# Moving the first block's GpSimd element-wise work to ScalarE and VectorE in a two-block fp32 kernel

## The chip, the cores and the metric

One core of one Trainium2 chip. The metric is the device time of one execution in microseconds (us); the kernel before took 2739.27 us (median of 3 runs, 2730.82 to 2743.38).

## What is computed

Two transformer-like blocks over 256 tokens of width 1024, in float32. The first block has two layers; each has three recurrent mixers (hgrn2 with 8 heads, retention with 8 heads, rwkv7 with 16 heads), every one of them run forwards and backwards, then three gated projections that are summed, and a residual. The second block has feed-forward layers, a short convolution and two kinds of attention; the change does not touch it. The part of the reference that matters here, cut:

```
for l in range(2):
    h = rmsnorm(x, norm_g[l])
    a_q, a_ff, ..., c_s, c_g, merge = split(h @ w_in[l])
    y_a = hgrn2_mixer(...) * silu(a_g)
    y_b = retention_mixer(...) * silu(b_g)      # head_groupnorm(o, g, b)
    y_c = rwkv7_mixer(...) * silu(c_g)          # head_groupnorm(o, ln_g, ln_b) + bonus
    gates = sigmoid(merge)
    mixed = gates_0*(y_a@w_a) + gates_1*(y_b@w_b) + gates_2*(y_c@w_c)
    x = x + mixed @ w_out[l]
```

## The kernel before

All large products are made at float32 accuracy out of three passes with split operands. `wload` (L350) brings 512 KB of weights into a `raw` tile over SP's queue; for each 128x512 piece ScalarE writes the rounded high part (`whi`, L411) and VectorE the rest (`wlo`, L412), and TensorE multiplies low by high, high by low and high by high (L370 to L372), 128x256 at a time. Such pieces have 4 pairs of buffers, and 1 more in the first block.

In the first block this stream of weights is the *fill*, and the recurrent mixers run beside it as chains of small steps. `weave` (L46) decides at build time when each chain's next step is written into the program, from written-down estimates of how long a step takes; then a scheduler sets the order of each engine's queue. Every engine works through its queue in order, so an instruction that waits holds up all that stand behind it. The chains are:

- rwkv7: 8 pairs of heads per layer. `rwkv_operands` makes the decays `eL`, `enL`, the keys `bk`, their decayed copy `bkP` and the sum `sqr` (called `ks` in the code) of both directions' keys; `rwkv_scores` makes `ar`, `UV`, the bonus `bv`, the score matrices `SCa`, `SCr` and their inverse (`XY`, `W`, `X`); `rwkv_states` runs the recurrence; `rwkv_out` makes the norm.
- hgrn2 and retention: `hgrn_pair`, `hgrn_head` and `ret_pair`, 4 pairs per layer each.
- `branch` multiplies a mixer's output by its projection and adds it to `mixed` (tile `gate`). After the last branch `layer` splits `mixed` into `hb` for the product with `w_out`.

GpSimd has, per layer: two copies `Pc` per rwkv7 pair (L957, L958), the sum `sqr` (L969), the two products `bkP` (L977), two copies each of `ar` and `UV` (through a helper, L105), the sum `onr` + `bv` (L1198); for hgrn2 `kf` (L1239 in layer 1, L1242 in layer 0), the product `EK` (L1292), two sums into `cm` (L1330, L1331) and four into `P` (L1351); for retention the gain and bias of the norm `ro` (L1440); and the sum into `mixed` (L895).

Of the kernel before, what the change touches and what calls it, by code (L numbers as in the profile page):

```python
# [13 lines left out]
AF = mybir.ActivationFunctionType  # L14
ALU = mybir.AluOpType
# [506 lines left out]
class First(Core):  # L522
# [355 lines left out]
    def branch(s, l, b, j, c, ys, st, parts=False):  # L878


        nc = s.nc
        sl = slice(2 * j, 2 * j + 2)
        gt, mixed = s.gates(b, j, st), st["gate", 0]
        p = s.bank("pb")
        if parts:
            yield from s.fm(p, c[:1], ys, open=True)
            yield from s.fm(p, c[1:], ys, cont=True)
        else:
            yield from s.fm(p, c, ys)
        if b == 0:  # L890
            nc.vector.scalar_tensor_tensor(gt, gt, 1.0, p, ALU.add, ALU.mult)
        else:
            t = s.tmp.tile([128, 2, T], F32, tag="gt", name="gb", bufs=1)
            nc.vector.scalar_tensor_tensor(t, gt, 1.0, p, ALU.add, ALU.mult)
            nc.gpsimd.tensor_tensor(mixed[:, sl, :], mixed[:, sl, :], t, ALU.add)  # L895

    def sums(s, out, fwd, bwd, n):

# [6 lines left out]
    def rwkv_operands(s, l, p, r, k, v, codes, out):  # L905
# [6 lines left out]
        col = lambda n: s.P(f"{n}{l}", p)  # L912
# [41 lines left out]
        A.activation(eL, csv, AF.Exp, scale=-EC)  # L954
        A.activation(enL, csv, AF.Exp, scale=EC)
        Pc = rp.tile([128, 2, 4], F32, tag="Pc", name="Pc", bufs=3)
        G.tensor_copy(Pc[:, 0, :], eL[:, 0, :, 63])  # L957
        G.tensor_copy(Pc[:, 1, :], eL[:, 1, :, 0])  # L958
        c4 = lambda t: t.rearrange("p (c t) -> p c t", c=4)
        bd = lambda t: c4(t).unsqueeze(1).to_broadcast([128, 2, 4, 64])  # L960
        bt = rp.tile([128, 2, 4, 64], F32, tag="cs", name="bt")
# [4 lines left out]
        A.activation(kd, ta4, AF.Identity, scale=s.ka1[l][:, 0, p:p + 1], bias=s.ka1[l][:, 1, p:p + 1])  # L966
        tt(kd, kd, bd(k), ALU.mult)
        ks = t1("sqr", 1)
        G.tensor_tensor(c4(ks), kd[:, 0], kd[:, 1], ALU.add)  # L969
        stt(ks, ks, col("rk"), r, ALU.mult, ALU.mult)  # L970
        stt(bk[:, :, :, 0, :], bt, -0.5, enL, ALU.mult, ALU.mult)
        A.copy(bk[64:128, :, :, 2, :], bk[64:128, :, :, 0, :])
# [1 line left out]

        bkP = rp.tile([128, 2, 3, 2, 64], F32, tag="A4", name="bkP")
        for d in range(2):
            G.tensor_tensor(bkP[:, d], bk[:, d, d:d + 3, 0:2, :],  # L977
                            Pc[:, d, d:d + 3].unsqueeze(2).unsqueeze(3).to_broadcast([128, 3, 2, 64]), ALU.mult)
        yield 220, 6000
        out[p] = vc, nkk, eL, Pc, bk, bkP, ks  # L980

    def rwkv_scores(s, l, p, r, v, ins, ev, wait):
# [3 lines left out]
        mm = nc.tensor.matmul  # L986
        tt = V.tensor_tensor
        vc, nkk, eL, Pc, bk, bkP, ks = ins
        c4 = lambda t: t.rearrange("p (c t) -> p c t", c=4)
        bd = lambda t: c4(t).unsqueeze(1).to_broadcast([128, 2, 4, 64])  # L990
        ar = rp.tile([128, 2, 4, 2, 64], F32, tag="ar", name="ar", bufs=2)
        n4 = c4(nkk)
        tt(ar[:, 0, :, 0, 1:], n4[:, :, 1:], eL[:, 0, :, :63], ALU.mult)
        G.tensor_copy(ar[:, 0, :, 0, 0:1], n4[:, :, 0:1])
        tt(ar[:, 1, :, 0, :63], n4[:, :, :63], eL[:, 1, :, 1:], ALU.mult)
        G.tensor_copy(ar[:, 1, :, 0, 63:64], n4[:, :, 63:64])
        tt(ar[:, :, :, 1, :], bd(r), eL, ALU.mult)
        ev.add(("r used", p))

# [1 line left out]
        for h in range(2):  # L1001
            o = (1 - h) * 64
            for i in range(2):
                A.copy(UV[o:o + 64, 0, i::2, h, :], vc[i * 64:i * 64 + 64, :, h, :])
            G.tensor_copy(UV[o:o + 64, 1, :, h, :], UV[o:o + 64, 0, :, h, :])
        yield wait
        bv = rp.tile([128, T], F32, tag="bv", name="bv", bufs=2)
        pb = mp.tile([128, T], F32, tag="m", name="pb")
        mm(out=pb, lhsT=s.blk, rhs=ks, start=True, stop=True)
        tt(bv, pb, v, ALU.mult)  # L1010
        ev.add(("v used", p))
        yield 480, 2500

# [172 lines left out]
    def rwkv_out(s, l, p, ins, cg):  # L1186

        V, tt = s.nc.vector, s.nc.vector.tensor_tensor
        on, sq, bv = ins
        col = lambda n: s.P(f"{n}{l}", p)  # L1190
        r4 = s.rp.tile([128, 4, 64], F32, tag="sqe", name="wide", bufs=1)
        s.columns(s.colps[:, 4:8], [[sq]], 2, 64.0, 64e-5, "rsr", out=r4)
        yield 220, 4000
        y = s.spread_wide(s.mps.tile([128, T], F32, tag="m", name="pn"), r4)
        yield 220, 0
        tt(on, on, y, ALU.mult)
        V.tensor_scalar(on, on, col("lg"), col("lb"), ALU.mult, ALU.add)
        s.nc.gpsimd.tensor_tensor(on, on, bv, ALU.add)  # L1198
        V.scalar_tensor_tensor(s.yc[:, p, :], on, 0.5, cg, ALU.mult, ALU.mult)


# [24 lines left out]
    def hgrn_pair(s, l, j, x, ys, ev):  # L1226
        nc, hp = s.nc, s.hp
        V, A = nc.vector, nc.scalar
        mm = nc.tensor.matmul
        has = lambda n: lambda: n in x  # L1230
        yield has("lf")
        lf = x["lf"]
        kf = hp.tile([128, 2, 2, T], F32, tag="kf", name="kf")
        for d, f in enumerate(lf):
            if l > 0:
                for h in range(2):
                    i = 8 * d + 2 * j + h
                    lb, om, nom = (s.lbc[:, m, i:i + 1] for m in range(3))
                    nc.gpsimd.tensor_scalar(kf[:, h, d, :], f[:, h, :], nom, om, ALU.mult, ALU.add)  # L1239
                    A.activation(f[:, h, :], f[:, h, :], AF.Identity, scale=om, bias=lb)  # L1240
            else:
                nc.gpsimd.tensor_scalar(kf[:, :, d, :], f, -0.5, 0.5, ALU.mult, ALU.add)  # L1242
                V.tensor_scalar(f, f, 0.5, 0.5, ALU.mult, ALU.add)
            V.tensor_scalar(f, f, 1e-6, None, ALU.max)
            A.activation(f, f, AF.Ln)
        yield 0, 4000
        po = s.hops.tile([128, 2, T], F32, tag="oh", name="hpo")
        for h in range(2):
            P = yield from s.hgrn_head(x, h, kf[:, h], [f[:, h, :] for f in lf], j, ev)
            yield has("v")  # L1250
            for jt in range(2):
                mm(out=po[:, h, :], lhsT=x["v"][:, h, jt, :], rhs=P[:, jt, :], start=jt == 0, stop=jt == 1)
            yield 860, 1000
        ev.add(("v used", j))
        sq = hp.tile([128, 2, T], F32, tag="Z", name="sqo")
        A.activation(sq, po, AF.Square)
        r = s.hmps.tile([128, 2, T], F32, tag="mh", name="hpn")
        c = s.columns(r.rearrange("p h t -> p (h t)"), [[sq[:, 0, :]], [sq[:, 1, :]]], 1, 128.0, 1e-6)
        yield 860, 3500
        s.spread(r, c, 1)  # L1260
        yield 440, 0
        y = hp.tile([128, 2, T], F32, tag="E", name="yo")
        for h in range(2):
            A.mul(y[:, h, :], po[:, h, :], s.P(f"hn{l}", 2 * j + h))
        yield has("g")
        g = x["g"]
        V.tensor_tensor(y, y, r, ALU.mult)
        V.scalar_tensor_tensor(y, y, 0.5, g, ALU.mult, ALU.mult)
        s.split(ys[0][:, 2 * j:2 * j + 2, :], ys[1][:, 2 * j:2 * j + 2, :], y)

    def hgrn_head(s, x, h, kf, lf, j, ev):
# [17 lines left out]
        EK = hp.tile([128, 2, T], F32, tag="Z", name="EK")  # L1289
        A.activation(EK, D, AF.Exp, scale=-1.0)  # L1290
        A.activation(D, D, AF.Exp, bias=s.eps[-SH])
        nc.gpsimd.tensor_tensor(EK, kf, EK, ALU.mult)  # L1292
        tt(D, q.unsqueeze(1).to_broadcast([128, 2, T]), D, ALU.mult)
        yield 0, 5500
        for d in range(2):
# [7 lines left out]
        for n in (8, 16, 32, 64, 128):  # L1303
# [21 lines left out]
            if n == 8:  # L1325
                for b in range(8):
                    sl, pp = slice(b * 32, b * 32 + 32), (b % 4) * 32
                    mm(out=pc[pp:pp + 32, b // 4, 0, :], lhsT=Z[:, 0, sl], rhs=Z[:, 1, sl], start=True, stop=True)
                tt(cm, pc, C["mh"].unsqueeze(1).to_broadcast([128, 2, 3, 32]), ALU.mult)
                nc.gpsimd.tensor_tensor(cm[:, :, 0, :], cm[:, :, 0, :], cm[:, :, 1, :], ALU.add)  # L1330
                nc.gpsimd.tensor_tensor(cm[:, :, 0, :], cm[:, :, 0, :], cm[:, :, 2, :], ALU.add)  # L1331
                pt = mp.tile([128, 2, T], F32, tag="mh", name="ppt")
            elif n == 16:
                for b in range(8):
                    sl, pp = slice(b * 32, b * 32 + 32), (b % 4) * 32
                    mm(out=pt[pp:pp + 32, b // 4, sl], lhsT=Z[:, 0, sl], rhs=Z[:, 1, sl], start=True, stop=True)
                yield 440, 0
            else:
                for b in range(g):
                    e, o = b * 2 * n, b * 2 * n + n  # L1340
                    for j0, i0 in ((e, o), (o, e)):
                        mm(out=pt[j0 % 128:j0 % 128 + n, j0 // 128, i0:i0 + n], lhsT=Z[:, 0, j0:j0 + n],
                           rhs=Z[:, 1, i0:i0 + n], start=True, stop=True)
                yield 440, 0
# [46 lines left out]
    def ret_pair(s, l, j, ins, st, new, ev):  # L1391
# [42 lines left out]
        for e in range(2):  # L1434
# [2 lines left out]
            tt(o[:, e], o[:, e], y[:, e, :].unsqueeze(1).to_broadcast([128, 2, T]), ALU.mult)  # L1437
            for vt in range(2):
                i = 2 * hd + vt
                G.tensor_scalar(o[:, e, vt, :], o[:, e, vt, :], s.P(f"rg{l}", i), s.P(f"rb{l}", i), ALU.mult, ALU.add)  # L1440
            V.scalar_tensor_tensor(o[:, e], o[:, e], 0.5, gt, ALU.mult, ALU.mult)
            b = (2 * hd) % 8
            s.split(ys[0][:, b:b + 2, :], ys[1][:, b:b + 2, :], o[:, e])
# [461 lines left out]
```

## Time and profile before

| what | value |
|---|---|
| median of 3 runs | 2739.27 us |
| the profiled execution | 2742.64 us, its span 2740.8 us |
| TensorE busy (matmul) | 2636.6 us, 96% |
| VectorE busy | 2068.3 us, 75% |
| ScalarE busy | 1494.7 us, 55% |
| GpSimd busy | 283.6 us, 10% |
| mean granted TensorE clock | 0.979 |

The first layer lies at about 0 to 850 us of the span, the second at 850 to 1700 us, the second block behind it. In the first 550 us of each layer the recurrent mixers run beside the weights (called the dense stages below, 50 to 550 us and 900 to 1400 us); behind them retention and the branches run beside the weights.

### The profile page before, as it was taken

Reading aid. Unit: us, or ns where it says so; the run is one execution under the profiler, and the core shown is the slowest. Engines: PE = TensorE matmul, PEld = TensorE weight load, DVE = VectorE, ACT = ScalarE, POOL = GpSimd, SP = SyncE. Lnnn points to the kernel's source line nnn. Section 1 sums busy time; section 2 is a strip of 40 time slices with the busy share of each in tenths; the row PEclk is TensorE's granted clock in tenths of the full one; section 3 lists DMA queues with packets and bytes.
Section 4 is the critical chain, followed back from the end, with each engine's and each line's share of the span. In section 5 each row is a group of like instructions: output and inputs, shape, how many; then the busy total and the mean of one; then the engine's idle time right before and its main releaser. Section 6 shows DMA issues by size and latency. Waiting matters only on the chain.

```text
span 2740.8 us, 76128 instructions
## 1 busy us (share of the span) xinstructions
PE 2636.6 (96%) x31971; PEld 2499.4 (91%) x31971; DVE 2068.3 (75%) x4578; ACT 1494.7 (55%) x2968; POOL 283.6 (10%) x385
## 2 busy tenths in 40 slices
PE   7999999999999899999999999999999999999999
PEld 7888888899999888888799999999999999987999
DVE  8988889866668988898967677766776767756665
ACT  6665646444456665656444455555555555554554
POOL 1111112101021222212100111000000000000000
PEclk9998999999999999999999999999999999998999
DMA  5332222244556332223245555556455655542555
GB/s 178 111 105 75 98 76 83 94 150 151 179 171 197 112 106 84 93 80 100 73 133 163 173 165 197 184 171 187 151 181 182 185 180 163 170 132 76 173 182 161
DMA packets 111800, 385.38 MB, mean 141 GB/s; under 512 B 12384, under 2 KB 16992, under 8 KB 111200
## 3 DMA queue, kind: packets, MB, share of 16 engines
q1 hardware_dynamic: 111024, 379.86, 42.9%
q8 instruction: 251, 4.11, 0.6%
q10 hardware_dynamic: 432, 0.64, 0.1%
q14 instruction: 93, 0.76, 0.1%
HBM read 378.36 MB, written 2.10 MB: 139 GB/s over the span
## 4 chain that ended last, share of the span: by engine, by line
PE 76%; DVE 16%; ACT 3%; issue 2%; POOL 1%; DMA 1%; SPq 0%; ACTq 0%; DVEq 0%; POOLq 0%
PE pj L370 7%; PE pj L372 6%; PE pj L371 6%; PE pg L370 4%; PE pg L372 4%; PE pg L371 4%; DVE wlo L412 4%; PE pw L370 3%; PE pw L372 3%; PE pw L371 3%; PE pu L370 3%; PE pu L372 3%; PE pu L371 3%; PE pb L370 2%; PE pb L371 2%; PE pb L372 2%
## 5 line engine op out<-in xcount | busy, mean ns | idle before, releaser
L411 ACT CAST whi<-raw 128x512 fp32r<-128x512 f32 (+1 forms) x1407 | 862.0, 618 | 825.3 <-PE pj L372 228.0
L412 DVE TENSOR_TENSOR wlo<-raw,whi 128x512 fp32r<-128x512 f32 (+1 forms) x1407 | 984.8, 707 | 422.0 <-ACT whi L411 412.4
L370 PE MATMUL pj<-hb,wlo 128*128 128x256 f32 x1408 | 425.3, 302 | 7.5 <-DVE wlo L412 7.1
L372 PE MATMUL pj<-hb,whi 128*128 128x256 f32 x1408 | 405.0, 288 | 0.0
L371 PE MATMUL pj<-hb,whi 128*128 128x256 f32 x1408 | 404.3, 287 | 0.0
L370 PEld LDWEIGHTS pj<-hb,wlo 128*128 128x128 f32 x1408 | 271.4, 193 | 19.5 <-DVE wlo L412 6.7
L371 PEld LDWEIGHTS pj<-hb,whi 128*128 128x128 f32 x1408 | 271.9, 193 | 1.9 <-issue 0.2
L372 PEld LDWEIGHTS pj<-hb,whi 128*128 128x128 f32 x1408 | 271.6, 193 | 1.4 <-issue 0.2
L371 PE MATMUL pg<-hs,whi 128*128 128x256 f32 x704 | 200.3, 284 | 2.0 <-DVE hs L499 2.0
L370 PE MATMUL pg<-hs,wlo 128*128 128x256 f32 x704 | 200.2, 284 | 1.5 <-DVE x L518 1.5
L370 PE MATMUL pu<-hs,wlo 128*128 128x256 f32 x704 | 199.9, 284 | 1.8 <-DVE wlo L412 1.6
L370 PE MATMUL pw<-g,wlo 128*128 128x256 f32 x704 | 199.6, 284 | 0.7 <-DVE wlo L412 0.7
L372 PE MATMUL pg<-hs,whi 128*128 128x256 f32 x704 | 200.2, 284 | 0.0
L372 PE MATMUL pu<-hs,whi 128*128 128x256 f32 x704 | 199.6, 283 | 0.0
L371 PE MATMUL pu<-hs,whi 128*128 128x256 f32 x704 | 199.3, 283 | 0.0
L371 PE MATMUL pw<-g,whi 128*128 128x256 f32 x704 | 199.2, 283 | 0.0
L372 PE MATMUL pw<-g,whi 128*128 128x256 f32 x704 | 199.2, 283 | 0.0
L370 PE MATMUL pb<-hs,wlo 128*128 128x256 f32 x512 | 145.3, 284 | 0.0
L371 PE MATMUL pb<-hs,whi 128*128 128x256 f32 x512 | 144.6, 282 | 0.0
L372 PE MATMUL pb<-hs,whi 128*128 128x256 f32 x512 | 144.6, 282 | 0.0
L371 PEld LDWEIGHTS pg<-hs,whi 128*128 128x128 f32 x704 | 135.7, 193 | 2.2 <-DVE hs L499 2.2
L370 PEld LDWEIGHTS pu<-hs,wlo 128*128 128x128 f32 x704 | 135.0, 192 | 2.6 <-DVE wlo L412 2.4
(526 smaller groups left out, 6852.8 us busy)
## 6 DMA issues: line engine op xcount, KB each, us to landing
raw<-in_win SPq DMA_DIRECT2D x292, 512.0 KB, 3.6
raw<-in_w SPq DMA_DIRECT2D x256, 512.0 KB, 3.6
raw<-in_wbb SPq DMA_DIRECT2D x32, 512.0 KB, 3.6
raw<-in_wo SPq DMA_DIRECT2D x32, 512.0 KB, 3.5
raw<-in_wconv SPq DMA_DIRECT2D x20, 512.0 KB, 3.6
raw<-in_wba SPq DMA_DIRECT2D x16, 512.0 KB, 3.5
raw<-in_wbc SPq DMA_DIRECT2D x16, 512.0 KB, 3.5
raw<-in_lora SPq DMA_DIRECT2D x16, 256.0 KB, 2.6
```

What stands on the lines that cost most here:

```text
L370: mm(out=out, lhsT=al, rhs=bh, start=start, stop=False)
L371: mm(out=out, lhsT=ah, rhs=bl, start=False, stop=False)
L372: mm(out=out, lhsT=ah, rhs=bh, start=False, stop=stop)
L411: s.nc.scalar.copy(dh, src)
L412: (eng or s.nc.vector).tensor_tensor(dl, src, dh.bitcast(F32), ALU.subtract)
```

## The change

GpSimd keeps only its start-up work. Copies (`Pc`, `ar`, `UV`), `bkP`, `kf` and the gain and bias of `ro` become ScalarE activations; `bkP` is six 128x128 activations with a per-partition factor in place of two products of 128x384. The sums and products (`sqr`, `EK`, `cm`, `P`, `mixed`) become VectorE instructions. The norm's bias is added to `bv` on ScalarE, right after `bv` is made, so that gain and sum of `onr` become one VectorE instruction in place of one on VectorE and one on GpSimd.

```diff
 branch:
-            nc.gpsimd.tensor_tensor(mixed[:, sl, :], mixed[:, sl, :], t, ALU.add)
+            nc.vector.tensor_tensor(mixed[:, sl, :], mixed[:, sl, :], t, ALU.add)
 rwkv_operands:
-        G.tensor_copy(Pc[:, 0, :], eL[:, 0, :, 63])
-        G.tensor_copy(Pc[:, 1, :], eL[:, 1, :, 0])
+        A.copy(Pc[:, 0, :], eL[:, 0, :, 63])
+        A.copy(Pc[:, 1, :], eL[:, 1, :, 0])
-        G.tensor_tensor(c4(ks), kd[:, 0], kd[:, 1], ALU.add)
+        tt(c4(ks), kd[:, 0], kd[:, 1], ALU.add)
-            G.tensor_tensor(bkP[:, d], bk[:, d, d:d + 3, 0:2, :],
-                            Pc[:, d, d:d + 3].unsqueeze(2).unsqueeze(3).to_broadcast([128, 3, 2, 64]), ALU.mult)
+            for c in range(3):
+                A.mul(bkP[:, d, c], bk[:, d, d + c, 0:2, :], Pc[:, d, d + c:d + c + 1])
 rwkv_scores:
+        lb = s.P(f"lb{l}", p)
-        G.tensor_copy(ar[:, 0, :, 0, 0:1], n4[:, :, 0:1])
+        A.copy(ar[:, 0, :, 0, 0:1], n4[:, :, 0:1])
-        G.tensor_copy(ar[:, 1, :, 0, 63:64], n4[:, :, 63:64])
+        A.copy(ar[:, 1, :, 0, 63:64], n4[:, :, 63:64])
-            G.tensor_copy(UV[o:o + 64, 1, :, h, :], UV[o:o + 64, 0, :, h, :])
+            A.copy(UV[o:o + 64, 1, :, h, :], UV[o:o + 64, 0, :, h, :])
         tt(bv, pb, v, ALU.mult)
+        A.activation(bv, bv, AF.Identity, bias=lb)
 rwkv_out:
-        V.tensor_scalar(on, on, col("lg"), col("lb"), ALU.mult, ALU.add)
-        s.nc.gpsimd.tensor_tensor(on, on, bv, ALU.add)
+        V.scalar_tensor_tensor(on, on, col("lg"), bv, ALU.mult, ALU.add)
 hgrn_pair:
-                    nc.gpsimd.tensor_scalar(kf[:, h, d, :], f[:, h, :], nom, om, ALU.mult, ALU.add)
+                    A.activation(kf[:, h, d, :], f[:, h, :], AF.Identity, scale=nom, bias=om)
-                nc.gpsimd.tensor_scalar(kf[:, :, d, :], f, -0.5, 0.5, ALU.mult, ALU.add)
+                A.activation(kf[:, :, d, :], f, AF.Copy, scale=-0.5, bias=0.5)
 hgrn_head:
-        nc.gpsimd.tensor_tensor(EK, kf, EK, ALU.mult)
+        tt(EK, kf, EK, ALU.mult)
-                nc.gpsimd.tensor_tensor(cm[:, :, 0, :], cm[:, :, 0, :], cm[:, :, 1, :], ALU.add)
-                nc.gpsimd.tensor_tensor(cm[:, :, 0, :], cm[:, :, 0, :], cm[:, :, 2, :], ALU.add)
+                tt(cm[:, :, 0, :], cm[:, :, 0, :], cm[:, :, 1, :], ALU.add)
+                tt(cm[:, :, 0, :], cm[:, :, 0, :], cm[:, :, 2, :], ALU.add)
-            nc.gpsimd.tensor_tensor(dst, dst, cm[i * 32:i * 32 + 32, :, 0, :], ALU.add)
+            tt(dst, dst, cm[i * 32:i * 32 + 32, :, 0, :], ALU.add)
 ret_pair:
-                G.tensor_scalar(o[:, e, vt, :], o[:, e, vt, :], s.P(f"rg{l}", i), s.P(f"rb{l}", i), ALU.mult, ALU.add)
+                A.activation(o[:, e, vt, :], o[:, e, vt, :], AF.Identity, scale=s.P(f"rg{l}", i), bias=s.P(f"rb{l}", i))
```

The change moves lines by one or two: `sqr` stays L969, `bkP` becomes L978, `EK` L1293, `P` L1352. The scheduler lays out all queues anew. On VectorE, at the keys of the second pair of heads in layer 0, the queue read, before:

```order
L947 SCALAR_TENSOR_TENSOR nkk<-t1r,pk 128x256
L967 TENSOR_TENSOR bk<-bk,rkv 128x8x64
L965 SCALAR_TENSOR_TENSOR bt<-sg,nkk 128x512
L970 SCALAR_TENSOR_TENSOR sqr<-sqr,par,rkv 128x256
L971 SCALAR_TENSOR_TENSOR bk<-bt,enL 128x8x64
L973 TENSOR_TENSOR bk<-bk,enL 128x8x64
```

and now reads:

```order
L947 SCALAR_TENSOR_TENSOR nkk<-t1r,pk 128x256
L967 TENSOR_TENSOR bk<-bk,rkv 128x8x64
L965 SCALAR_TENSOR_TENSOR bt<-sg,nkk 128x512
L969 TENSOR_TENSOR sqr<-bk 128x256
L971 SCALAR_TENSOR_TENSOR bk<-bt,enL 128x8x64
L970 SCALAR_TENSOR_TENSOR sqr<-sqr,par,rkv 128x256
L973 TENSOR_TENSOR bk<-bk,enL 128x8x64
```

The sum L969 stands in the queue itself, and one instruction lies between it and L970, which reads it.

On ScalarE, at the same pair of heads, from the decays to the copy of the keys (`whi` are the casts of the weights), before:

```order
L954 ACTIVATE eL<-cs 128x512
L955 ACTIVATE enL<-cs 128x512
L966 ACTIVATE bk<-sg,ka_188 128x8x64
L1319 ACTIVATE E<-E 128x512
L411 CAST whi<-raw 128x512
L858 ACTIVATE g<-pj 128x512
L411 CAST whi<-raw 128x512
L972 COPY bk<-bk 64x8x64
L411 CAST whi<-raw 128x512
```

and now:

```order
L954 ACTIVATE eL<-cs 128x512
L955 ACTIVATE enL<-cs 128x512
L957 COPY Pc<-eL 128x4
L958 COPY Pc<-eL 128x4
L966 ACTIVATE bk<-sg,ka_188 128x8x64
L411 CAST whi<-raw 128x512
L105 COPY ar<-nkk 128x4 x2
L858 ACTIVATE g<-pj 128x512
L411 CAST whi<-raw 128x512
L972 COPY bk<-bk 64x8x64
L411 CAST whi<-raw 128x512
L978 ACTIVATE bkP<-bk,Pc 128x128 x6
```

Four short copies and the six `bkP` activations stand in the queue that casts the weights. GpSimd's queue goes from 240 rows to 30, those of the start-up.

## Rows read from the trace of the kernel before

**Rows 1.** The page's part 1: busy time, share, instructions of each engine

```profile
PE 2636.6 (96%) x31971; PEld 2499.4 (91%) x31971; DVE 2068.3 (75%) x4578; ACT 1494.7 (55%) x2968; POOL 283.6 (10%) x385
```

**Rows 2.** Windows: stretch, length, PE, PEld, DVE, ACT, POOL busy, PEclk, DMA share, GB/s

```profile
50.00:550.00 500.00, 468.93 (x9097) 420.05 (x9095) 435.76 (x1099) 286.93 (x618) 89.03 (x143) 0.96 0.29 92
550.00:850.00 300.00, 296.85 (x2443) 290.64 (x2438) 204.56 (x363) 141.65 (x266) 44.22 (x33) 0.99 0.50 164
...
900.00:1400.00 500.00, 469.99 (x9155) 420.45 (x9154) 434.12 (x1100) 296.33 (x641) 101.49 (x151) 0.98 0.29 94
```

**Rows 3.** The page's part 4: the chain that ended last, by engine

```profile
PE 76%; DVE 16%; ACT 3%; issue 2%; POOL 1%; DMA 1%; SPq 0%; ACTq 0%; DVEq 0%; POOLq 0%
```

**Rows 4.** The chain from 96 to 102 us: start us, us, what

```profile
97.22 0.74 POOL sqr L969
...
100.01 0.96 DVE Z L1321
```

**Rows 5.** The timeline from 99 to 104 us: start us, us, instruction

```profile
99.84 1.82 POOL L977 TENSOR_TENSOR bkP<-bk,Pc 128x384 f32<-128x384 f32 x2 [1.89 <-ACT bk L972]
99.92 1.05 DVE L1321 TENSOR_TENSOR Z<-q,E 128x256 f32<-128x256 f32 x1
...
101.23 0.97 DVE L412 TENSOR_TENSOR wlo<-raw,whi 128x512 fp32r<-128x512 f32 x1
```

**Rows 6.** Groups of GpSimd, whole span: busy us, mean ns, idle before, releaser

```profile
L895 POOL TENSOR_TENSOR gate<-gate,gb 128x512 f32<-128x512 f32 x32 | 53.3, 1666 | 183.8 <-DVE gb L894 183.8
L1440 POOL TENSOR_SCALAR ro<-ro,par 128x256 f32<-128x256 f32 x32 | 33.6, 1064 | 312.6 <-DVE ro L1437 312.6
L977 POOL TENSOR_TENSOR bkP<-bk,Pc 128x384 f32<-128x384 f32 x32 | 33.0, 1049 | 28.3 <-DVE bk L973 19.7 <-DVE bk L971 4.7 <-ACT bk L972 3.8
L1351 POOL TENSOR_TENSOR P<-P,cm 32x64 f32<-32x64 f32 x64 | 28.4, 444 | 181.3 <-DVE P L1347 168.4 <-DVE rs L446 10.1
L1292 POOL TENSOR_TENSOR EK<-kf,EK 128x512 f32<-128x512 f32 x16 | 22.5, 1406 | 134.5 <-ACT EK L1290 71.7 <-issue 34.0 <-ACT UV L105 28.5
...
L969 POOL TENSOR_TENSOR sqr<-bk 128x256 f32<-128x256 f32 x16 | 13.5, 844 | 5.4 <-PE pn L478 2.6 <-DVE bk L967 1.6 <-PE pw L1081 0.7
```

**Rows 7.** Groups of VectorE from the first block (the last row: the second block)

```profile
L412 DVE TENSOR_TENSOR wlo<-raw,whi 128x512 fp32r<-128x512 f32 x672 | 478.5, 720 | 127.1 <-ACT whi L411 122.7
L1318 DVE TENSOR_TENSOR E<-S 128x256 f32<-128x256 f32 x48 | 23.4, 487 | 0.0
L1268 DVE SCALAR_TENSOR_TENSOR yo<-yo,g 128x512 f32<-128x512 f32 x8 | 7.1, 892 | 0.0
L973 DVE TENSOR_TENSOR bk<-bk,enL 128x512 f32<-128x512 f32 x16 | 10.9, 682 | 0.0
L493 DVE TENSOR_TENSOR acc<-acc,sq 128x256 f32<-128x256 f32 x28 | 11.5, 417 | 0.3 <-ACT sq L491 0.2
L412 DVE TENSOR_TENSOR hb<-gate,hb 128x256 fp32r<-128x256 f32 x16 | 11.0, 691 | 4.0 <-ACT hb L411 4.0
...
L412 DVE TENSOR_TENSOR wlo<-raw,whi 128x512 fp32r<-128x512 f32 x629 | 431.5, 691 | 263.9 <-ACT whi L411 259.7
```

**Rows 8.** Waits of VectorE, first block: us in total, times, longest us

```profile
DVE sqr L970 <- POOL sqr L969: 8.0, 13, 1.1
```

**Rows 9.** Groups of ScalarE from the first block

```profile
L411 ACT CAST whi<-raw 128x512 fp32r<-128x512 f32 x672 | 411.5, 618 | 348.9 <-PE pj L372 211.1 <-PE pb L372 56.3 <-PE pg L372 40.1
L105 ACT COPY X<-XY 32x256 f32<-32x256 f32 x64 | 25.8, 403 | 10.0 <-DVE XY L105 9.5
L1240 ACT ACTIVATE lf<-lf,lbc 128x256 f32<-128x256 f32 x16 | 9.5, 600 | 6.2 <-POOL kf L1239 6.0
L916 ACT ACTIVATE t1r<-rkv,par 128x256 f32<-128x256 f32 x16 | 8.1, 505 | 1.0 <-DVE nkk L947 0.5 <-DVE rkv L628 0.4
```

**Rows 10.** The timeline at the end of layer 0, at the last sum into `mixed`

```profile
839.31 1.48 DVE L412 TENSOR_TENSOR hb<-gate,hb 128x256 fp32r<-128x256 f32 x1
```

**Rows 11.** Waits of TensorE, first block: us in total, times, longest us

```profile
PE pj L370 <- DVE wlo L412: 18.0, 8, 11.0
```

## The prediction

> **What bounds the kernel now.** I read the page's engine shares first, then the busy time by stages, then the chain that ended last, and only then single groups. TensorE is busy for 2636.6 of 2740.8 us and GpSimd for 283.6 [rows 1]; the matmuls don't change, so anything to win lies in stretches where TensorE waits or creeps. The stages say where: in the two dense stages TensorE is busy for 469 and 470 us of 500 and VectorE for 436 and 434, ScalarE for 287 and 296; behind them TensorE has 297 of 300 and VectorE 205 [rows 2]. So in the dense stages VectorE stands at 87%, close behind TensorE, and elsewhere everything but TensorE has slack. The chain agrees: 76% TensorE, 16% VectorE, 3% ScalarE, 1% GpSimd [rows 3]. GpSimd is seldom the last to finish, but it costs in two ways. VectorE waits for it: the chain runs through the sum `sqr` on GpSimd for 0.74 us [rows 4], and VectorE sat idle for `sqr` for 8.0 us in all [rows 8]. And VectorE's own instructions are longer beside it: while GpSimd makes `bkP` (1.82 us from 99.84), `Z` takes 1.05 us and a `wlo` 0.97 us [rows 5], where 128x256 with both inputs in SBUF takes 0.417 and `wlo` 0.691 us with GpSimd idle [rows 7]. That `Z` is a piece of the chain [rows 4].
>
> **What the change does to VectorE's load.** Added: 32 sums into `mixed` and 16 `EK`, 128x512, at 0.682 us [rows 7] are 21.8 and 10.9 us; 16 `sqr` at 0.417 [rows 7] are 6.7; the 32 sums into `cm` and 64 into `P` are small, bounded by 0 and the 0.417 of 128x256, and I take half, 0.2, so 19.2. The joined gain and sum in `rwkv_out` replaces one VectorE instruction of the same size: nothing. Sum 58.6 us, of which 36.8 in the dense stages (all but `mixed`).
>
> Taken away, by groups: `wlo` 720 ns against 691 in the second block where GpSimd does nothing, 672 times, is 19.5 us; `E` 487 against 417, 48 times, 3.4; `yo` 892 against 682, 8 times, 1.7; `hb` 691 against 417, 16 times, 4.4 [rows 7]. That is 29.0 us over the groups shown, 24.6 without `hb`, which lies at the layers' ends; with the 8.0 us of idle time for `sqr`, 32.6. Against 36.8 added, VectorE's load in the dense stages stays about where it was. The gain, if there is one, is not less work on VectorE but shorter steps on the chain, and relief that falls where VectorE is the one that is late.
>
> **The sum on the path.**
> - GpSimd's pieces on the chain: 1% of the span is 27 us (14 to 41, as the page rounds). Their replacements take about half: `sqr` 844 ns becomes 417, `P` 444 becomes some 200, `mixed` 1666 becomes 682, `ro` 1064 becomes the 600 of a ScalarE activation with factor and bias [rows 6, 7, 9]. So **-13 us** (-7 to -20).
> - Lengthened VectorE instructions: the chain holds 16% of 2741 = 439 us of VectorE's 2068, or 21%. If contention were spread like the rest, 21% of 24.6 = 5 us would come off; if it all lay on the chain, 24.6. GpSimd's bursts come at the keys of a pair, where the chain does run on VectorE [rows 4, 5], so I take half: **-12** (-5 to -25).
> - New VectorE work on the chain, beside what the first item prices: `EK` 10.9 and `cm` 6.4, at 21%: **+4** (0 to +17).
> - The two layer ends: the last split `hb` took 1.48 us beside GpSimd [rows 10] against 0.417, and TensorE waits for it in both layers: **-2**.
> - ScalarE: 96 `bkP` of 128x128, bounded by nothing and the 0.505 us of 128x256 with a factor [rows 9]; I take 0.35, above the half, since a small instruction is not free: 33.6 us. 32 `ro` and 16 `kf` at 0.600, 8 `kf` of 128x512 at 0.618, 16 `bv` at 0.505, 32 `UV` at 0.403 [rows 9], and 64 copies of four columns at 0.2 (between 0 and 0.403): 28.8 + 4.9 + 8.1 + 12.9 + 12.8. Together 101 us on an engine that has 287 of 500 in the dense stages [rows 2]. What hides it: the casts `whi` sit idle for 349 us in the first block, nearly all until TensorE gives buffers back [rows 9], so weights are split well ahead; and TensorE's largest wait for `wlo` is 18.0 us, 11.0 of it in one go [rows 11]. ScalarE holds 3% of 2741 = 82 us of the chain out of its 1495, 5.5%, and at that share 101 us cost **+6** (0 to +34, the slower rival).
> - The sums into `mixed` lie in stages where VectorE has 205 of 300 [rows 2]: nothing. Without that cover they would cost up to their 21.8. The retention norm on ScalarE, in the same stages: nothing.
>
> Sum -13 -12 +4 -2 +6 = -17 on the profiled execution's 2742.6, or 2725.6. That execution lies 3.4 us above the median of the runs, so I forecast **2722 us**. With `sqr` and `bkP` gone from GpSimd, what is late next at a pair's keys is VectorE itself with its 0.68 us products.
>
> A rule to weigh: the rows show a `Z` lengthened by 0.63 us and a `wlo` by 0.28 beside 1.82 us of `bkP` [rows 5], 0.91 in all, or 14.6 for the 16 pairs. The Trainium skill (SBUF — State Buffer, Who interferes with whom) says that GpSimd and a VectorE instruction with two SBUF inputs take an exclusive lock on a shared port pair, the later one waiting until the first is done. By it each pair could lose all 1.82 us, 29 us in 16 pairs; here half of that shows. The measured half stands in my sum.
>
> **The rivals.**
> 1. *All the contention lay on the chain*: -24.6 in place of -12, and ScalarE's work hidden, 0 in place of +6: -35, so 2704. For it: the row on the chain that is the lengthened one [rows 4, 5]. Against: `wlo`, the largest group, is mostly ahead of its need [rows 11]. 15%. The lock in the Trainium skill's SBUF page, cited above, would point this way.
> 2. *No change*: VectorE's load is the same as before, and what comes off the chain uncovers a neighbour a fraction of a us later. Contention -5, GpSimd's pieces -7, layer ends -2, new VectorE work +4, ScalarE +6: -4, so 2735. For it: the near-equal ledger of 36.8 against 32.6. 29%.
> 3. *Slower, through ScalarE's queue*: the six `bkP` stand among the casts and wait for VectorE's products of the keys; GpSimd's separate queue could wait at no one's cost, and did, 28.3 us [rows 6]. If the split weights run out there, each pair's 6 x 0.35 = 2.1 us reach TensorE: 16 pairs, +34. With -13 -5 -2 +4 that is +18, so 2757. It decides once the casts lose their idle time; against it stand those 349 us [rows 9]. 18%.
>
> That the change does not do what it says I rule out: GpSimd's queue is left with its start-up instructions.
>
> **How the numbers follow.** The forecast has 38%, with a range of its own of 2708 to 2732. About 0.5% (13.7 us) is what a measurement of this kernel can tell from no change: under 2725.6 is faster, over 2753.0 slower. Faster is rival 1 and four fifths of the forecast: 0.15 + 0.31 = 0.46; the same is the rest of the forecast and rival 2: 0.07 + 0.29 = 0.36; slower is rival 3: 0.18. The range goes from 2697 (rival 1 and some of what the clock held back: 0.96 in the first dense stage [rows 2] is 40 us at the lower level of 1.2 GHz, costing 20 at most) to 2752; beyond it lie most of rival 3's upper half and little below, some 15%.
>
> **What would show it.** Right: `wlo` in the first block near 691 ns, `E` near 417, `hb` after the last branch near 417; VectorE's busy time within 35 us of 2068 (58.6 added, 29.0 or more removed); ScalarE near 1596; GpSimd gone from the chain; TensorE's waits for VectorE in the dense stages shorter. Wrong on prices: `bkP` far from 0.35 us, `P` from 0.2. Wrong on the path: `whi` casts waiting for nothing but ScalarE itself, waits of TensorE for `wlo` well over 18 us, or dense stages as long as before with all instructions shorter.

## The result, and the profile after

The changed kernel takes **2698.04 us** (median of 6 runs, 2684.58 to 2704.23) against 2737.92 for the kernel before (6 runs, 2722.16 to 2743.38): a ratio of 0.9847, interval 0.9819 to 0.9874, so 39.9 us faster. The forecast was 2722, a gain of 17 us; the range of 2697 to 2752 holds the result, close to its lower end. The profiled execution is the slowest of the six, 2704.23 us, span 2702.4, mean granted clock 0.983.

The page's part 1, as in [rows 1], and the engines' shares of the chain that ended last, as in [rows 3]:

```profile
PE 2621.1 (97%) x31971; PEld 2488.1 (92%) x31971; DVE 2064.6 (76%) x4738; ACT 1570.9 (58%) x3232; POOL 4.4 (0%) x25
...
PE 77%; DVE 14%; ACT 5%; DMA 2%; issue 2%; ACTq 0%; DVEq 0%; SPq 0%
```

VectorE has 160 instructions more and is busy for 3.7 us *less*. ScalarE is busy for 76.2 us more.

The stretches of [rows 2] (length, PE, PEld, DVE, ACT, POOL busy, granted clock, DMA share, GB/s):

```profile
50.00:550.00 500.00, 478.92 (x9305) 429.64 (x9304) 441.42 (x1192) 321.38 (x745) 0.00 (x0) 0.98 0.30 96
550.00:850.00 300.00, 297.11 (x2413) 293.08 (x2412) 214.21 (x398) 156.81 (x298) 0.00 (x0) 0.99 0.55 176
...
900.00:1400.00 500.00, 479.64 (x9312) 433.90 (x9312) 436.38 (x1168) 321.83 (x739) 0.00 (x0) 0.97 0.31 99
```

In the first dense stage TensorE does 9305 matmuls where it did 9097, in the second 9312 for 9155.

The same work on the chain: the keys of a pair, from the chain's rows at 95 to 99 us (start us, us, what). The sum `sqr` now holds 0.34 us of the chain on VectorE itself, and no GpSimd stands in the chain as it did in [rows 4]:

```profile
95.60 0.34 DVE sqr L969
95.94 0.60 DVE bk L971
96.54 0.40 DVE sqr L970
96.93 0.60 DVE bk L973
97.53 0.34 DVE E L1314
97.87 0.34 DVE E L1319
```

VectorE's groups in the first block, as in [rows 7] (busy us, mean ns, idle before). `wlo` fell from 720 to 687 ns, `E` from 487 to 415, `hb` from 691 to 418:

```profile
L412 DVE TENSOR_TENSOR wlo<-raw,whi 128x512 fp32r<-128x512 f32 x694 | 471.7, 687 | 132.8 <-ACT whi L411 126.4 <-issue 0.3
...
L895 DVE TENSOR_TENSOR gate<-gate,gb 128x512 f32<-128x512 f32 x32 | 21.9, 685 | 0.0
L1319 DVE TENSOR_TENSOR E<-S 128x256 f32<-128x256 f32 x48 | 19.9, 415 | 0.0
L1352 DVE TENSOR_TENSOR P<-P,cm 32x64 f32<-32x64 f32 x64 | 13.6, 213 | 0.9
L1293 DVE TENSOR_TENSOR EK<-kf,EK 128x512 f32<-128x512 f32 x16 | 10.9, 681 | 0.1
L969 DVE TENSOR_TENSOR sqr<-bk 128x256 f32<-128x256 f32 x16 | 6.7, 419 | 0.1
L412 DVE TENSOR_TENSOR hb<-gate,hb 128x256 fp32r<-128x256 f32 x16 | 6.3, 418 | 0.0
...
L1331 DVE TENSOR_TENSOR cm<-cm 128x64 f32<-128x64 f32 x16 | 3.5, 218 | 0.0
L1332 DVE TENSOR_TENSOR cm<-cm 128x64 f32<-128x64 f32 x16 | 3.5, 218 | 0.0
```

The added work is 21.9 + 10.9 + 6.7 + 13.6 + 7.0 = 60.1 us. As the total fell by 3.7, about 64 us of VectorE's time went away elsewhere; the prediction's ledger had 29.0.

ScalarE's groups, as in [rows 9]. The six `bkP` of a pair cost 389 ns each and the engine waited 1.1 us for all 96 of them; the casts `whi` still have 328 us of idle time, nearly all until TensorE gives buffers back:

```profile
L978 ACT ACTIVATE bkP<-bk,Pc 128x128 f32<-128x128 f32 x96 | 29.8, 389 | 1.1 <-DVE bk L973 0.9
L1441 ACT ACTIVATE ro<-ro,par 128x256 f32<-128x256 f32 x32 | 17.8, 592 | 0.0
...
L411 ACT CAST whi<-raw 128x512 fp32r<-128x512 f32 x694 | 424.4, 617 | 328.4 <-PE pj L372 203.4 <-PE pb L372 59.9 <-PE pg L372 34.2
```

(Of `ro`, `bkP` and the casts alike, busy time is less than count times mean where instructions overlap.)

**Where the 38.4 us between the two spans lie.** The product with `w_out` ends each layer. Windows from its first to its last matmul, in both layers, in the kernel before:

```profile
834.80:861.70 26.90, 24.59 (x192) 24.30 (x192) 21.82 (x41) 15.32 (x33) 3.18 (x2) 0.94 0.73 223
1677.60:1704.50 26.90, 24.59 (x193) 24.30 (x192) 22.71 (x45) 17.47 (x39) 3.18 (x2) 0.94 0.59 196
```

and in the changed kernel:

```profile
812.90:835.40 22.50, 22.50 (x193) 22.50 (x192) 17.55 (x39) 13.55 (x30) 0.00 (x0) 1.00 0.72 220
1640.40:1662.90 22.50, 22.50 (x193) 22.50 (x192) 19.68 (x44) 16.44 (x37) 0.00 (x0) 1.00 0.66 214
```

Their bounds give the table (the code of the second block is the same in both kernels):

| stretch | before | after | difference |
|---|---|---|---|
| layer 0 up to the product with `w_out` | 834.8 | 812.9 | -21.9 |
| that product | 26.9 | 22.5 | -4.4 |
| layer 1 up to it (1677.6 - 861.7, 1640.4 - 835.4) | 815.9 | 805.0 | -10.9 |
| that product | 26.9 | 22.5 | -4.4 |
| the second block (2740.8 - 1704.5, 2702.4 - 1662.9) | 1036.3 | 1039.5 | +3.2 |

So 33 us come from the layers' bodies and 8.8 from two short stretches at their ends.

Where in the bodies: each body is cut at the last matmul of its recurrent chains, which is at the same number of matmuls in both kernels. In the kernel before:

```profile
0.00:569.50 569.50, 526.48 (x9570) 474.69 (x9571) 484.54 (x1229) 327.71 (x703) 93.66 (x168) 0.96 0.32 103
861.70:1412.20 550.50, 518.58 (x9573) 466.72 (x9571) 472.43 (x1197) 326.51 (x701) 101.49 (x151) 0.97 0.31 99
```

and in the changed kernel:

```profile
0.00:548.00 548.00, 515.25 (x9570) 465.09 (x9570) 479.84 (x1293) 354.80 (x815) 4.35 (x25) 0.98 0.33 107
835.40:1375.60 540.20, 515.82 (x9573) 466.60 (x9572) 472.96 (x1264) 359.52 (x823) 0.00 (x0) 0.97 0.32 102
```

These two stretches, the dense stages with a little more at each end, are 21.5 and 10.3 us shorter, which is all but 1 us of what the bodies gave. In them VectorE's busy time fell by 4.2 us in all and its idle time by 27.6, from 163.0 to 135.4. VectorE does 38.2 us of added work there (all but `mixed`), so some 42 us of its other work went away.

Why the ends: the sums into `mixed` and the splits of it in the last us of layer 0, and the matmul that needs the split, in the kernel before (start us, us, instruction, idle before it):

```profile
838.93 1.58 POOL L895 TENSOR_TENSOR gate<-gate,gb 128x512 f32<-128x512 f32 x1 [2.43 <-DVE gb L894]
839.31 1.48 DVE L412 TENSOR_TENSOR hb<-gate,hb 128x256 fp32r<-128x256 f32 x1
840.85 0.39 PE L371 MATMUL po<-hb,whi 128*128 128x256 f32 x1 [2.31 <-DVE hb L412]
```

and the same splits in the changed kernel:

```profile
815.19 0.76 DVE L412 TENSOR_TENSOR hb<-gate,hb 128x256 fp32r<-128x256 f32 x2
816.46 0.76 DVE L412 TENSOR_TENSOR hb<-gate,hb 128x256 fp32r<-128x256 f32 x2
```

In both layers of the kernel before TensorE waits once within the product, 2.31 us for a split `hb` that VectorE makes while GpSimd adds into `mixed`; in the changed kernel it doesn't wait there at all. Behind that wait some of its matmuls follow each other after 0.21 us in place of 0.12, the lower of its two clock levels: the granted clock of the product is 0.94, and 1.00 in the changed kernel. The wait is 2.3 of the 4.4 us and the slower matmuls 2.1 (24.59 us busy for 22.50). All runs in which GpSimd still makes this sum for the kernel show this wait of 2.3 us in both layers; the runs with the sum on VectorE and no other work for GpSimd beside it show none.

### The profile page after: what moved, and what is told of

The parts are those of the page before. It is cut to its first block, busy times and chain, and to the rows that moved or that the text cites. A ratio compares the mean times of both kernels' runs of the same rounds, so it can differ in the third digit from the quotient of the medians.

```text
span 2702.4 us, 75967 instructions
## 1 busy us (share of the span) xinstructions
PE 2621.1 (97%) x31971; PEld 2488.1 (92%) x31971; DVE 2064.6 (76%) x4738; ACT 1570.9 (58%) x3232; POOL 4.4 (0%) x25
## 4 chain that ended last, share of the span: by engine, by line
PE 77%; DVE 14%; ACT 5%; DMA 2%; issue 2%; ACTq 0%; DVEq 0%; SPq 0%
PE pj L370 7%; PE pj L371 6%; PE pj L372 6%; PE pg L370 4%; PE pg L372 4%; PE pg L371 4%; PE pu L370 3%; PE pw L370 3%; PE pw L372 3%; PE pw L371 3%; PE pu L372 3%; DVE wlo L412 3%; PE pu L371 3%; PE pb L370 2%; PE pb L371 2%; PE pb L372 2%
## 5 line engine op out<-in xcount | busy, mean ns | idle before, releaser
L412 DVE TENSOR_TENSOR wlo<-raw,whi 128x512 fp32r<-128x512 f32 (+1 forms) x1407 | 959.4, 688 | 419.5 <-ACT whi L411 407.8
L371 PEld LDWEIGHTS pj<-hb,whi 128*128 128x128 f32 x1408 | 269.2, 191 | 2.6 <-DVE hb L412 1.1
L372 PEld LDWEIGHTS pj<-hb,whi 128*128 128x128 f32 x1408 | 268.7, 191 | 1.2
L370 PEld LDWEIGHTS pg<-hs,wlo 128*128 128x128 f32 x704 | 136.3, 194 | 2.1 <-issue 2.1
```

What stands on the lines that cost most here:

```text
L370: mm(out=out, lhsT=al, rhs=bh, start=start, stop=False)
L371: mm(out=out, lhsT=ah, rhs=bl, start=False, stop=False)
L372: mm(out=out, lhsT=ah, rhs=bh, start=False, stop=stop)
L412: (eng or s.nc.vector).tensor_tensor(dl, src, dh.bitcast(F32), ALU.subtract)
```

## The experiments

All times are medians; ratios are to the kernel before, measured beside each experiment. A gain over the kernel before is taken from the ratio, a distance from the changed kernel from the medians; by the ratios the distances of experiments 6 to 9 would be 1 to 5 us longer. Where GpSimd is given extra work, it goes into a tile that nobody reads.

**1. Only `bkP`** (kernel before, `bkP` on ScalarE).

```diff
-            G.tensor_tensor(bkP[:, d], bk[:, d, d:d + 3, 0:2, :],
-                            Pc[:, d, d:d + 3].unsqueeze(2).unsqueeze(3).to_broadcast([128, 3, 2, 64]), ALU.mult)
+            for c in range(3):
+                A.mul(bkP[:, d, c], bk[:, d, d + c, 0:2, :], Pc[:, d, d + c:d + c + 1])
```

> The kernel before with bkP alone on ScalarE, all else left on GpSimd. Theory A (the gain is VectorE no longer lengthened beside GpSimd): bkP lengthened VectorE by some 0.9 us per pair, 16 pairs, at points where VectorE is late: 10 to 15 us faster than before. Theory B (the gain is the hand-overs to and from GpSimd that go): nobody waits for bkP, so no change within 4 us. Theory C (the gain is the new order that the scheduler finds, whatever moved): anything from -20 to +20, without a tie to the lengthening.

Measured: 2729.02, ratio 0.9964 (0.9939 to 0.9989), 10 us faster. GpSimd lost 31 us and VectorE, of whose instructions none was touched, 12.5:

```profile
PE 2614.9 (96%) x31971; PEld 2481.7 (91%) x31971; DVE 2055.8 (76%) x4578; ACT 1520.9 (56%) x3064; POOL 252.3 (9%) x353
```

That is some 0.4 us of VectorE per us of GpSimd; `E`, for one, took 426 ns for 487. It fits theory A, that this time lay on the path. The gain alone doesn't show it, as it is no larger than what a new layout can do (experiment 10).

**2. Only the sum into `mixed`** (kernel before, L895 on VectorE).

```diff
-            nc.gpsimd.tensor_tensor(mixed[:, sl, :], mixed[:, sl, :], t, ALU.add)
+            nc.vector.tensor_tensor(mixed[:, sl, :], mixed[:, sl, :], t, ALU.add)
```

> The kernel before with the sum into mixed alone on VectorE; TensorE's order is the same as before. Theories A and B both: the two layer ends shorten by 3 to 4 us each, 6 to 8 in all, and nothing else, though GpSimd's largest lengthening of VectorE (L895) is gone, since VectorE has slack there. My sum on record gave these ends 2 us plus a share of the GpSimd pieces. C: no change, as the order is the same.

Measured: 2729.2, 0.9957 (0.9936 to 0.9978), 12 us faster by the ratio and 8 by the medians. The product with `w_out` takes 22.5 us in both layers, as in the changed kernel, and TensorE doesn't wait in it: the 8.8 us belong to this line.

**3. and 4. Two inputs or one.** Experiment 3 moves only the instructions with two input tiles (`sqr`, `bkP`, `onr`, `EK`, `cm`, `P`, `mixed`), experiment 4 only those with one (`Pc`, `ar`, `UV`, `kf`, `ro`); together they are the change. One line of experiment 3:

```diff
-        nc.gpsimd.tensor_tensor(EK, kf, EK, ALU.mult)
+        tt(EK, kf, EK, ALU.mult)
...
```

and of experiment 4:

```diff
-            G.tensor_copy(UV[o:o + 64, 1, :, h, :], UV[o:o + 64, 0, :, h, :])
+            A.copy(UV[o:o + 64, 1, :, h, :], UV[o:o + 64, 0, :, h, :])
...
```

> The kernel before with the instructions of two inputs moved as in the change (sqr, bkP, bv and onr, EK, cm, P, mixed), and Pc, ar, UV, kf and ro left on GpSimd. A: nearly the whole gain, 32 to 40 us. B: half to two thirds, since Pc, kf and ro are still handed over. C: anything.

> The kernel before with the instructions of one input moved as in the change (Pc, ar, UV, kf, ro to ScalarE), and the two-input ones left on GpSimd. A: no gain, 0 to 6 us slower through ScalarE's 50 us of added work. B: 8 to 15 us faster. C: no change, as TensorE's order is nearly the same.

Measured: experiment 3 2699.69, 0.9865 (0.9831 to 0.9899), 37 us faster, nearly the whole gain. Its part 1:

```profile
PE 2609.5 (97%) x31971; PEld 2479.1 (92%) x31971; DVE 2072.2 (77%) x4738; ACT 1526.0 (57%) x3078; POOL 108.8 (4%) x177
```

GpSimd still works for 108.8 us, and VectorE is only 7.6 us above the changed kernel: beside the 60.1 us added, 56.2 were freed (2068.3 + 60.1 - 2072.2). So VectorE is busy for 3.9 us more than in the kernel before, and the kernel is 37 us faster all the same. The run does not decide between the theories, since most hand-overs went with the two-input work too: of VectorE's waits for GpSimd, 16.1 us in all in the kernel before (`sqr` 8.0, `ro` 3.5, `onr` 3.6, `kf` 1.0), 3.6 are left. Experiment 4: 2722.79, 0.9945 (0.9919 to 0.9972), 15 us faster, which missed the theory that I held. `E` stays longer there, and VectorE's wait for GpSimd's `sqr` goes from 8.0 us [rows 8] to 4.6:

```profile
L412 DVE TENSOR_TENSOR wlo<-raw,whi 128x512 fp32r<-128x512 f32 x688 | 484.8, 712 | 135.3 <-ACT whi L411 130.5
...
L1318 DVE TENSOR_TENSOR E<-S 128x256 f32<-128x256 f32 x48 | 22.4, 466 | 0.0
```

```profile
DVE sqr L970 <- POOL sqr L969: 4.6, 9, 0.6
```

Theory A gave this run no gain, but either mechanism can have made it: VectorE's waits for GpSimd fell by 9.2 us, and its busy time by 10.0 (2058.3), though none of its instructions was touched. The two gains don't add up (37 + 15 for 40): once the two-input work has left GpSimd, the one-input moves are worth almost nothing.

**5. GpSimd repeats its work for nobody** (changed kernel; `mixed`, `bkP` and `EK` made a second time on GpSimd).

```diff
+                nc.gpsimd.tensor_tensor(s.idle, kf[:, i, o], EK[:, i, o], ALU.mult)
...
+                    nc.gpsimd.tensor_tensor(s.idle, mixed[:, 2 * j + i, o], t[:, i, o], ALU.add)
...
```

> The changed kernel with GpSimd repeating bkP, EK and the sum into mixed into a scratch tile that nobody reads, in pieces of 128x128 with two inputs. No result of GpSimd is waited for; only VectorE's lengthening comes back (and the buffers that GpSimd reads are given back later). A: 15 to 25 us slower than the changed kernel, some 2713 to 2723. B: as the changed kernel, 2698. C: anything, as the order changes.

Measured: 2732.0, 0.9981 (0.996 to 1.0001), 34 us lost. But the extra sum reads `t`, which has one buffer, and VectorE waited for that:

```profile
DVE gb L895 <- POOL idle L899: 37.8, 22, 2.0
```

So this run doesn't show contention alone. Experiment 9 leaves that part out.

**6. and 7. Where `bkP` belongs** (changed kernel, `bkP` back on GpSimd; on VectorE).

```diff
-            for c in range(3):
-                A.mul(bkP[:, d, c], bk[:, d, d + c, 0:2, :], Pc[:, d, d + c:d + c + 1])
+            tt(bkP[:, d], bk[:, d, d:d + 3, 0:2, :],
+               Pc[:, d, d:d + 3].unsqueeze(2).unsqueeze(3).to_broadcast([128, 3, 2, 64]), ALU.mult)
```

That is experiment 7; experiment 6 has `G.tensor_tensor` in place of `tt`.

> The changed kernel with bkP back on GpSimd. A: 10 to 15 us slower than the changed kernel, 2708 to 2713. B: as the changed kernel, or a few us faster, since ScalarE loses 37 us of work.

> The changed kernel with bkP on VectorE, as two products of 128x384 (32 at some 0.55 us, 17.6 us) in place of 96 ScalarE instructions (37 us). If VectorE is what bounds the dense stages (A): 5 to 15 us slower than the changed kernel. If ScalarE's added work costs (rival 3 of the prediction): faster by as much.

Measured: 2708.6, 0.9904 (0.9865 to 0.9942), and 2709.23, 0.99 (0.9873 to 0.9926); both 11 us above the changed kernel and above all its layouts (2698 to 2704, experiments 11 and 15), though their intervals touch its own. So `bkP` on GpSimd cost as much as on VectorE itself. That fits VectorE as the engine that is late at a pair's keys; nothing here shows ScalarE late.

**8. and 9. One input or two, beside the same VectorE work** (changed kernel with extra work on GpSimd: 288 instructions with one input; 160 with two, `bkP` and `EK` again).

```diff
+                nc.gpsimd.tensor_scalar(s.idle, EK[:, i, o], 2.0, None, ALU.mult)
...
```

The line of experiment 8 above stands in experiment 9 as

```diff
+                nc.gpsimd.tensor_tensor(s.idle, kf[:, i, o], EK[:, i, o], ALU.mult)
...
```

> The changed kernel with GpSimd running tensor_scalar of one input into a scratch tile, as many and of the same size as in the run with two inputs. A with a lengthening by every GpSimd instruction that reads SBUF: as slow as the run with two inputs. A with a lengthening by two-input GpSimd instructions alone: within 4 us of the changed kernel. B: as the changed kernel.

> As the run in which GpSimd repeated work of two inputs, but without the sum into mixed, whose reading held back the one buffer that VectorE writes next (37.8 us of VectorE's waits there). Only bkP and EK are repeated, in the dense stages; nobody waits for them. A (VectorE lengthened): 8 to 18 us slower than the changed kernel. B (hand-overs): within 4 us of it.

Measured: experiment 8 2702.35, 0.9878 (0.9858 to 0.9898), 4 us above the changed kernel, with an interval that overlaps its own; experiment 9 2711.94, 0.9903 (0.9869 to 0.9937), 14 above, with an interval that just touches. Part 1 of experiment 8 and of experiment 9:

```profile
PE 2614.8 (97%) x31971; PEld 2483.6 (92%) x31971; DVE 2075.5 (77%) x4738; ACT 1573.3 (58%) x3232; POOL 210.5 (8%) x313
```

```profile
PE 2629.4 (97%) x31971; PEld 2497.8 (92%) x31971; DVE 2082.7 (77%) x4738; ACT 1572.8 (58%) x3232; POOL 107.4 (4%) x185
```

Beside the changed kernel's 2064.6, 206 us of one-input work lengthened VectorE by 10.9 us (5%), 103 us of two-input work by 18.1 (18%). Layouts move these busy times by 3 us at most (2067.4 to 2069.9 in experiments 10 and 14 and the kernel before, 2064.2 to 2064.6 in experiments 11 and 15 and the changed kernel), so both lengthenings are clear. The times of the kernels are less so: the two runs differ in layout as well, which the next runs price.

**10, 11, 14 and 15. The layout alone.** One of the planner's written estimates, changed in the kernel before (10, 14) and in the changed one (11, 15). The work is the same; only the order in the queues differs.

```diff
-        yield 220, 6000
+        yield 220, 5000
```

In experiments 14 and 15 the number is 7000.

> The kernel before with one of the planner's estimates changed (the rest after rwkv_operands 5000 in place of 6000), so that the queues are laid out anew with the same work. C (the order makes the gain): it moves by 10 us or more either way. A and B: within 6 us of the kernel before.

> The changed kernel with the same planner's estimate changed. C: it moves by 10 us or more either way, to 2688 or 2708. A and B: within 6 us of the changed kernel.

> The kernel before with the planner's estimate moved the other way (7000 in place of 6000): a third layout of the same work. If the layout is worth some 10 us by chance (C as a part), it falls anywhere between 2725 and 2750; if the kernel before was an unlucky layout, it is again near 2729.

> The changed kernel with the estimate at 7000. If the changed kernel was a lucky layout: 2705 to 2712. If not: 2692 to 2704.

| estimate | 5000 | 6000 | 7000 | mean |
|---|---|---|---|---|
| work as before | 2729.62 | 2737.92 | 2737.87 | 2735.1 |
| work as changed | 2703.0 | 2698.04 | 2704.08 | 2701.7 |

Ratios in the order of the labels: 0.9958 (0.9941 to 0.9974), 0.9857 (0.9822 to 0.9893), 1.0006 (0.9997 to 1.0015), 0.9876 (0.9859 to 0.9893). One of the four new layouts, experiment 10, moved its kernel by 8 us (medians) to 11 (ratio), beyond the 6 that theories A and B allow; the other three moved theirs by 0 to 6. So a layout can be worth some 10 us by itself. Every layout of the changed work beats every layout of the old; over the three the gain is 33.4 us, so by that estimate some 6 of the 40 are this layout's luck. In the profiled executions TensorE's idle time (span less busy time) is 104 to 113 us in the three old layouts and 73 to 85 in the three new ones, 29 less in the mean, while its busy time has the same mean (2624.6 and 2623.4): what the change saves is waiting of TensorE.

**12 and 16. More onto ScalarE** (changed kernel; two scalings moved from VectorE to ScalarE, `sg` in both layers and `lf` in layer 0; in 16 the second one is folded into the logarithm behind it).

```diff
-                ts(sw, sw, 0.5, 0.5, ALU.mult, ALU.add)
+                A.activation(sw, sw, AF.Copy, scale=0.5, bias=0.5)
-                V.tensor_scalar(f, f, 0.5, 0.5, ALU.mult, ALU.add)
+                A.activation(f, f, AF.Copy, scale=0.5, bias=0.5)
```

That is experiment 12; in experiment 16 the last line is

```diff
+                V.tensor_scalar(f, f, 2e-6 - 1.0, None, ALU.max)
+                A.activation(f, f, AF.Ln, scale=0.5, bias=s.eps[0.5])
+                continue
```

> The changed kernel with two scalings moved from VectorE to ScalarE (sg, 16 x 0.43 us, and lf in layer 0, 8 x 0.42 us; 0.63 us each on ScalarE). If VectorE is still what is late in the dense stages: 3 to 8 us faster than the changed kernel, 2690 to 2695. If ScalarE has become as late: no change or slower.

> The run that moved two scalings to ScalarE, and in layer 0 the scaling of lf folded into the logarithm's own factor and bias, so that neither engine has it. If VectorE is still late in the dense stages: 4 to 9 us faster than the changed kernel, 2689 to 2694. If the gain is used up: 2698.

Measured: 2692.29, 0.9832 (0.9802 to 0.9862), and 2698.26, 0.9839 (0.982 to 0.9858). Both intervals overlap that of the changed kernel, and both differences are smaller than a layout's: no version better than the changed one is shown.

**13. Only `sqr`** (kernel before, the sum L969 on VectorE).

```diff
-        G.tensor_tensor(c4(ks), kd[:, 0], kd[:, 1], ALU.add)
+        tt(c4(ks), kd[:, 0], kd[:, 1], ALU.add)
```

> The kernel before with the sum sqr alone on VectorE, where VectorE waited 8.0 us for GpSimd. B (hand-overs): 6 to 12 us faster than before. A (lengthening): within 3 us, since sqr lengthened VectorE by under 1 us in all and its own 6.7 us take the place of the 8.0 of waiting.

Measured: 2731.34, 0.9975 (0.9954 to 0.9995), 6 us faster, at the border of the two theories and within a layout's 10 us: unclear. VectorE is busy for 5.7 us more there (2074.0).

## Why the prediction was right and wrong

The direction, the place and the prices held; the sum was less than half of what came. One term is shown to have been sized wrong, the layer ends; those for the dense stages were too small together, and how they divide stays open.

- **What bounds the kernel: right.** TensorE keeps its matmuls, and in the dense stages it went from 469 and 470 us of 500 to 479 and 480. Some 32 of the 38 us between the spans lie up to the end of the recurrent chains, where VectorE is nearly full.
- **Prices: right.** `bkP` 389 ns for 350, `P` 213 and `cm` 218 for 200, `mixed` 685, `EK` 681 and `sqr` 419 as taken. `wlo` 687 for 691, `E` 415 for 417, `hb` 418 for 417. For `bkP`, where I took a middle between bounds, the Trainium skill (ScalarE: Activation LUTs, What ACT_TABLE_LOAD costs) has the price: 186 ns and 0.833 per element of a row, and 93 for each per-partition operand, by which 128 elements with one factor are an estimated 386 ns; the trace agrees with 389.
- **"The two layer ends: -2": the step that is shown to have failed, by its size.** They gave 8.8, and experiment 2 gives the same 8.8 by one line. The mechanism was right, TensorE does wait for `hb`. But I priced the split by its own lengthening, about 1 us each, where TensorE's whole wait was 2.3 us in each layer and the lower clock behind it cost 2.1 more.
- **"VectorE's load stays about where it was": right, by an error in both halves of the ledger.** In the stretches that end with the recurrent chains it is busy for 4.2 us less. Freed there were some 42 us for 24.6, against 38.2 added for 36.8; over the whole kernel about 64 for 29.0, against 60.1 for 58.6. The ledger took four groups with conspicuous means and passed over many that are longer by less, like `E` of L1313, 452 ns before and 413 after, 80 times. And its `wlo` was that of all stages: behind the dense ones, where VectorE has slack, `wlo` was as long (725 and 723 ns) as within them (731 and 723).
- **"Lengthened VectorE instructions: -12", "GpSimd's pieces on the chain: -13", new work +4 and ScalarE +6: together too small.** They make -15 (some of it for `mixed` and `ro`, behind the dense stages); the stretches that end with the recurrent chains gave -31.8. That there was lengthening is shown (experiments 1, 8 and 9), and experiment 9 puts a price on it without any hand-over: 18.1 us of VectorE, and 14 of the kernel (8 above the slowest layout of the changed one). But the change also puts 38.2 us of new work on VectorE, so shorter instructions beside it make only 4.2 us of less work; the other 27.6 us are idle time of VectorE that went. Of that, 12.5 are its waits for GpSimd in these stretches. Here too the ledger was short. It had the 8.0 of `sqr` [rows 8], where VectorE waited for GpSimd for 16.1 us in all; the other waits for GpSimd in the kernel before were, besides those of the layer ends (us in total, times, longest us):

```profile
DVE ro L1441 <- POOL ro L1440: 3.5, 8, 0.5
DVE bv L105 <- POOL onr L1198: 2.3, 2, 1.3
DVE yc L1199 <- POOL onr L1198: 1.3, 2, 0.6
DVE lf L1243 <- POOL kf L1242: 1.0, 1, 1.0
...
ACT lf L1240 <- POOL kf L1239: 6.0, 6, 1.4
...
PE hpo L1252 <- POOL P L1351: 4.7, 2, 2.4
```

None of them is left in the changed kernel. What ended the rest of VectorE's idle time no run shows; shorter steps on the chain, as predicted, would do it.
- **"ScalarE: +6": no run shows this cost.** It took 76 us more, for 101, and the casts kept 328 of their 349 us of idle time. Taking `bkP` off ScalarE made the kernel slower (experiments 6 and 7), and giving it two of VectorE's scalings made it no slower (experiment 12). Rival 3 falls: its condition, casts without idle time, never came. ScalarE's share of the chain did go from 3% to 5%.
- **What the misses come to.** With -8.8 for -2 and nothing for +6, the sum of -17 would have been some -30, and with the layout's 6 some -36. The 4 us that are left of the 40 are the error of the terms for lengthening, hand-overs and new work, taken together. This is an estimate: no run prices them one by one.
- **Rival 1**, all the contention on the chain and ScalarE hidden, gave 2704, nearly the time, with 15%. The runs fit its half on ScalarE. That all the contention lay on the chain is not shown, and the time is in part luck: its 24.6 came from the short ledger, and it had the ends at -2. Its "against", that `wlo` is ahead of its need, held: TensorE's wait for `wlo` hardly moved, 14.9 us for 18.0 [rows 11].

```profile
PE pj L370 <- DVE wlo L412: 14.9, 4, 10.7
```

- **The rule of the Trainium skill** (SBUF — State Buffer, Who interferes with whom): a VectorE instruction with two SBUF inputs contends with a GpSimd instruction that reads SBUF, for a port pair that one of them holds alone. In direction it spoke for this change, and experiment 9 agrees, though with 18% of GpSimd's time and not all of it. Experiment 8 agrees more weakly: GpSimd with one SBUF input at a time cost VectorE 5%, `hb` took 483 ns for 418, and `E` stayed at 414 there (423 in experiment 9):

```profile
L1327 DVE TENSOR_TENSOR E<-S 128x256 f32<-128x256 f32 x48 | 19.9, 414 | 0.0
```

- **Not in the sum: layout and clock.** Some 6 us are the layout's. At the granted clock of 0.984 one run of the changed kernel took 2699.71 and runs of the kernel before 2731 to 2738, so 32 to 38 us at equal clock for 40 between the medians.

Open is how the 32 us of the dense stages divide between shorter VectorE instructions and hand-overs that went away. Experiments 3 and 4 are not additive, experiment 13 is unclear, and experiment 9 has a layout of its own.

## What to carry to other kernels

Before an element-wise operation with two inputs is left on GpSimd to spare a VectorE that is nearly full, compare VectorE's *total* busy time with and without it, over all groups: here 175 us of it on GpSimd (283.6 - 108.8, experiment 3) cost VectorE 56 us, and doing it there cost 60. So the work on GpSimd spared VectorE next to nothing, and its hand-overs came on top. One-input work on GpSimd, once the two-input work was gone from there, and ScalarE, where its casts sit idle, were nearly free. Price the last instruction of a stage by the whole wait of the engine that needs it and by the clock behind that wait, not by its own length, and test an edit on two or three layouts of the queues, since a layout alone moved the time by up to some 10 us here.

## What was not expected of the hardware

- Lengthening depends on GpSimd's operands: 10.9 us on VectorE for 206 us of one-input instructions, 18.1 for 103 us of two-input ones (experiments 8 and 9); 12.5 for the 31 us of `bkP` (experiment 1), which ran right beside the products of the keys.
- GpSimd's one-input instruction is no shorter than its two-input one. The groups of experiment 8 and of experiment 9, 128x128 each (busy us, mean ns):

```profile
L1301 POOL TENSOR_SCALAR idle<-EK 128x128 f32<-128x128 f32 x64 | 45.6, 713 | 281.5 <-DVE EK L1298 277.6
```

```profile
L1299 POOL TENSOR_TENSOR idle<-kf,EK 128x128 f32<-128x128 f32 x64 | 42.8, 669 | 298.8 <-DVE EK L1296 295.1
```

- A gap of 2.3 us of TensorE cost nearly twice itself, as the clock fell with it: the product with `w_out` was busy for 24.59 us at 0.94 and for 22.50 at 1.00, so of its 4.4 us 2.3 were the gap and 2.1 the clock.
